# Split-operand products and a new strand order in the second mixer of a two-block transformer

## The chip, the cores and the metric

The kernel runs on one core of a Trainium2 chip. The metric is the device time of one execution in microseconds (us). Five engines work beside each other, each on its own queue: PE (TensorE, matrix products; its weight loads are counted apart as PEld), DVE (VectorE), ACT (ScalarE), POOL (GpSimd) and SP (SyncE, which issues the DMAs).

## The reference

Two blocks of two layers each run one after the other over a sequence of 512 tokens of width 1024, in float32. Each layer is a mixer and a feed-forward part; the first block has a cross-attention in between. The change touches one mixer, that of the first block's second layer. Cut to what matters:

```
proj = rms_norm(h) @ cd_w_in
lru_x, lru_g, m_x, m_o, m_if = split_cols(proj)

# y_a, gated linear recurrence, 512 channels in 4 blocks of 128
xc = causal_dwconv(lru_x, 4 taps)
r_gate, i_gate = sigmoid(xc_block @ gate_w[0 or 1] + gate_b)
log_a = -8 * r_gate * softplus(-lam)
u = sqrt(-expm1(2 * log_a)) * (i_gate * xc)
y_a = linear_recurrence(exp(log_a), u) * gelu(lru_g)

# y_b, matrix-memory head, 4 heads of 128 channels
xc = silu(causal_dwconv(m_x, 4 taps))
q, k = headwise(xc, w[0]), headwise(xc, w[1]) * 128 ** -0.5
v = headwise(m_x, w[2])
w = exp(log_d - max) * (q k^T), causal; num = w v; den = sum(w)
y_b = sigmoid(m_o) * norm(num / max(|den|, ...))

h = h + concat(y_a, y_b) @ w_mix_out
```

## The kernel before

Activations lie channel-major: a tile has 128 channels on the partitions and the 512 tokens along the free axis. A weight matrix is loaded in blocks of 128 output channels. A dense product is done as a **three-pass product** (`mm3`): each operand is split into a high part, rounded to the type `float32r`, and the remainder, and high x high, high x low and low x high are summed in PSUM. Products of smaller size are plain float32 (`mm`), which the profile shows as two records each. Splitting (`split`) is a cast on ACT and a subtraction on DVE:

```
def mm3(self, out, w, x, start, stop):
    wh, wl = w
...
    xh, xl = x
    self.mm(out, wh, xh, start, False)
    self.mm(out, wh, xl, False, False)
    self.mm(out, wl, xh, False, stop)
def split(self, src, n=T):
    hi, lo = self.big(F32R), self.big(F32R)
    self.nc.scalar.copy(out=hi[:, :n], in_=src[:, :n])
    self.tt(lo[:, :n], src[:, :n], hi[:, :n].bitcast(F32), SUB)
```

The mixer in question is `mixer_cd`. Its input projection has 17 blocks of 128 outputs: 0 the gates of the heads, 1 to 4 their input (`xm`, and after convolution and SiLU `xc`), 5 to 8 the output gate `so`, 9 to 12 the recurrence's input (after convolution `xl`), 13 to 16 its outer gate `gl`. One **dense step** is one three-pass product of 512 columns; a block has eight of them, as has each pair of blocks of a product over half the channels (`mix_out`, `kb=4`). Blocks 0, 1, 5 and 2 are the opening, under which the mean square of the input is finished.

Then `weave` takes over. It runs two **strands** at a time, each a Python generator that yields after each small piece of work: a head (`mlstm_head`: queries, keys, values, scores in four causal strips of 512, 384, 256 and 128 columns, numerator, statistics, output; 15 strand steps) or the recurrence (`rglru`: eight gate products, then exponentials, logarithms and scans; 20 strand steps). A strand starts when the other one has made 6 steps. After each strand step 1.75 dense steps of the **filler** are taken (`CD = (1.75, 6, 1)`). The filler of before is: the remaining nine blocks (`CDF[1]`, in the order 6, 3, 7, 4, 8, 9 to 12), the last part of the memory's values for the coming cross-attention (16 dense steps), blocks 13 to 16, and, once all four heads are done, the half of the output product that takes the heads' results `yb`. The strands are heads 0 to 3 and then the recurrence. What is left of the filler follows, and last comes the closing half of the output product, which takes the recurrence's result `ya`, adds the residual and prepares the next stage.

The order written in the code is a priority, not the final order of each queue: the framework's scheduler lets a later instruction go ahead of an earlier one that it expects to wait. Tiles of 128 x 512 lie in 84 shared slots (`NBIG`) that are handed on in the order in which they come free. Most instructions carry the line of a helper: L485 is every product, L475 every tensor-tensor operation, L472 every activation, L514 the cast of a loaded weight, L501 the cast of `split`, L513 a weight's DMA, L1733 the recurrence's scan.

Of the kernel before, what the change touches and what calls it, by code (L numbers as in the profile page):

```python
# [7 lines left out]
F32 = mybir.dt.float32  # L8
F32R = mybir.dt.float32r
# [8 lines left out]
T = 512  # L18
HT = T // 2
P = 128  # L20
# [327 lines left out]
class Builder:  # L348
# [1286 lines left out]
    def mlstm_head(self, h, xm, xc, rT, M, o, out):  # L1635
        nc = self.nc
        qkv = self.sm['qkv']
        hs = slice(h * P, (h + 1) * P)
        q, k, v = self.big(), self.big(), self.big()
        ps = self.ax_ps()  # L1640
        self.mm(ps, qkv[0][:, hs], xc)
        self.copy(q, ps)
        yield
        ps = self.ax_ps()
        self.mm(ps, qkv[1][:, hs], xc)
        self.act(k, ps, AF.Copy, scale=128 ** -0.5)
        yield
        ps = self.ax_ps()
        for t in range(4):
            self.mm(ps[:, t * P:(t + 1) * P], xm[:, 3 + t * P:3 + (t + 1) * P], qkv[2][:, hs])  # L1650
        self.copy(v, ps, 's')
        yield
        Mb = self.ax_ps()
        self.mm(Mb, self.c('ident')[0:4, h:h + 1].to_broadcast([4, P]), M[0:4])
        W, wsum = [], self.big()
        for sb in range(4):
            n = T - sb * P
            w = self.big()
            self.ts(w[:, :n], Mb[:, sb * P:], rT[:, 4 * sb + h:4 * sb + h + 1], SUB, 0.0, MAX)
            W.append(w)  # L1660
        yield
        for sb in range(4):
            n = T - sb * P
            w = W[sb]
            self.act(w[:, :n], w[:, :n], AF.Exp, scale=-1.0)
            self.tt(w[:, :P], w[:, :P], self.c('causal'), MULT, nc.gpsimd)
            sc = self.ax_ps()
            self.mm(sc[:, :n], k[:, sb * P:(sb + 1) * P], q[:, sb * P:])
            self.tt(w[:, :n], sc[:, :n], w[:, :n], MULT)
            if sb == 0:  # L1670
                self.copy(wsum, w, 's')
            else:
                self.tt(wsum[:, sb * P:], wsum[:, sb * P:], w[:, :n], ADD, nc.gpsimd)
            yield
        num = self.ax_ps()
        for sb in range(4):
            self.mm(num[:, sb * P:], v[:, sb * P:(sb + 1) * P], W[sb][:, :T - sb * P], sb == 0, sb == 3)
            yield
        sq, hn = self.big(), self.big()
        self.act(sq, num, AF.Square)  # L1680
        self.ts(hn, num, self.v('mng', h), MULT)
        st = self.ax_ps()
        for i, src in enumerate((wsum, sq)):
            for t in range(4):
                self.mm(st[:, 4 * i + t:4 * i + t + 1], src[:, t * P:(t + 1) * P], self.c('ones')[:, 0:1])
            yield
        d = self.small([P, 16], tag='mld')
        self.copy(d[:, 0:8], st[:, 0:8])
        self.stt(d[:, 8:12], d[:, 0:4], -1.0, d[:, 0:4], MULT, MAX)
        eT = rT[:, 16:32].rearrange("p (t h) -> p h t", h=4)[:, h]  # L1690
        self.tt(d[:, 8:12], d[:, 8:12], eT, MAX)
        self.stt(d[:, 8:12], d[:, 8:12], EPS, d[:, 8:12], MULT, MULT)
        self.stt(d[:, 8:12], d[:, 4:8], 1.0 / P, d[:, 8:12], MULT, ADD)
        self.tt(d[:, 12:16], d[:, 8:12], self.c('mhalf')[:, :4], ALU.pow, nc.gpsimd)
        yield
        self.tt(hn, hn, self.bcast(d[:, 12:16]), MULT)
        self.tt(hn, hn, o, MULT, nc.gpsimd)
        out[h] = self.split(hn)

    def rglru(self, xl, gl, lru, sp, out):  # L1700
        nc = self.nc
        rg, ig, th = [], [], []
        for n in range(4):
            cs = slice(n * P, (n + 1) * P)
            for dst, g in ((rg, 0), (ig, 1)):
                ps = self.ax_ps()
                self.mm(ps, lru[g][:, cs], xl[n])
                t = self.big()
                self.act(t, ps, AF.Sigmoid, bias=self.v(f'lgb{g}', n))
                dst.append(t)  # L1710
                yield
            t = self.big()
            self.act(t, rg[n], AF.Tanh, scale=sp[:, n:n + 1])
            self.ts(t, t, 1e-18, MAX)
            th.append(t)
            self.tt(ig[n], ig[n], xl[n], MULT, nc.gpsimd)
        for n in range(4):
            l = self.big()
            self.act(l, th[n], AF.Ln, bias=self.c('one'))
            self.act(th[n], th[n], AF.Ln, scale=2.0)  # L1720
            self.tt(th[n], th[n], l, SUB)
            yield CD[2]
        for n in range(4):
            self.act(th[n], th[n], AF.Exp, scale=0.5)
            self.act(rg[n], rg[n], AF.Exp, scale=sp[:, 4 + n:5 + n])
            self.tt(ig[n], ig[n], th[n], MULT)
            yield CD[2]
        for n in range(4):
            while n not in gl:
                yield  # L1730
            self.act(gl[n], gl[n], AF.Gelu_apprx_tanh)
            hh = self.big()
            nc.vector.tensor_tensor_scan(out=hh, data0=rg[n], data1=ig[n], initial=0.0, op0=MULT, op1=ADD)  # L1733
            self.tt(hh, hh, gl[n], MULT, nc.gpsimd)
            out[n] = self.split(hh)
            yield CD[2]

    def mixer_cd(self, filler, nxt):
        norm = self.norm_end()
        xs = self.xg  # L1740
        self.sm['qkv'] = [self.load_part('s_qkv', i) for i in range(3)]
        lru = [self.load_part('s_lru', i) for i in range(2)]
        sp = self.small([P, 16], tag='sp')
        c = self.vat['lam']
        lam = self.vec[:, c:c + 4]
        self.act(sp[:, 0:4], lam, AF.Abs)
        self.act(sp[:, 0:4], sp[:, 0:4], AF.Exp, scale=-1.0)
        self.act(sp[:, 0:4], sp[:, 0:4], AF.Ln, bias=self.c('one'))
        self.ts(sp[:, 4:8], lam, -1.0, MULT, 0.0, MAX)
        self.tt(sp[:, 0:4], sp[:, 0:4], sp[:, 4:8], ADD)  # L1750
        self.ts(sp[:, 4:8], sp[:, 0:4], -8.0, MULT)
        self.ts(sp[:, 0:4], sp[:, 0:4], 8.0, MULT)
        xm, xc, so, xl, gl, st, ya, yb = {}, {}, {}, {}, {}, {}, {}, {}

        def emit(n, ps):
            if n == 0:
                st['g'] = self.mlstm_gates(ps)
            elif n < 5:
                xm[n - 1] = self.evac_pad(ps, 3)
                xc[n - 1] = self.conv4(xm[n - 1], 'mcw', 'mcb', n - 1)  # L1760
                self.act(xc[n - 1], xc[n - 1], AF.Silu)
            elif n < 9:
                t = so[n - 5] = self.big()
                self.tt(t, ps, self.R, MULT)
                self.act(t, t, AF.Sigmoid)
            elif n < 13:
                xl[n - 9] = self.conv4(self.evac_pad(ps, 3), 'lcw', 'lcb', n - 9)
            else:
                t = gl[n - 13] = self.big()
                self.tt(t, ps, self.R, MULT)  # L1770

        def proj(blocks, groups=None):
            return self.dense_steps([self.ap['w_cd'][n] for n in blocks], xs, lambda b, ps: emit(blocks[b], ps),
                                    groups=groups)

        def mix_out(y, a, emit, groups=None, **kw):
            return self.dense_steps([self.ap['w_mo'][1][n][:, a:a + T] for n in range(8)], y, emit, groups=groups, kb=4, **kw)

        def fill():
            yield from chain(proj(CDF[1], [1] * len(CDF[1])))  # L1780
            yield from filler
            yield from chain(proj(range(13, 17), [1] * 4))
            while len(yb) < 4:
                yield
            yield from chain(mix_out([yb[h] for h in range(4)], T, self.partial))

        def head(h):
            while h not in so or h not in xc or 'g' not in st:
                next(more)
            yield from self.mlstm_head(h, xm[h], xc[h], *st['g'], so[h], yb)  # L1790

        def gated():
            while len(xl) < 4:
                next(more)
            yield from self.rglru(xl, gl, lru, sp, ya)
        more = fill()
        self.opening(proj(CDF[0], CDF[2]), norm, AT)
        self.weave([head(h) for h in range(4)] + [gated()], more, CD[0], CD[1])
        lockstep(more)
        lockstep(mix_out([ya[n] for n in range(4)], 0, self.resid(nxt), GO, closing=True))  # L1800

    def load_part(self, name, i):
        t = self.big()
# [597 lines left out]
```

## Time and profile before

| | |
|---|---|
| time, median of 3 runs | 2987.32 us (2980.75 to 2989.16) |
| the profiled execution | 2984.35 us, span 2982.2 us, mean granted clock 0.998 |
| PE busy | 2939.2 us |
| DVE busy | 2184.4 us |
| ACT busy | 1472.6 us |
| POOL busy | 240.5 us |
| HBM read | 259.53 MB, 88 GB/s over the span |

The profile is of one execution. An engine's busy time is the time covered by its instructions; a product's end is modelled, so a busy PE isn't a PE at its peak. PE's weight loads (PEld) run ahead under the products.

### The profile page before, as it was taken

The page shows a single profiled execution, that of the slowest core. Times are in us where ns is not written, and L with a number is a line of the kernel's source. Part 1 is how long each engine was busy: PE and PEld are TensorE (multiplying, and loading weights), DVE is VectorE, ACT ScalarE, POOL GpSimd, SP SyncE. Part 2 cuts the span into 40 slices and gives each one's busy share as a digit, 9 for nine tenths or more (in the row PEclk, how much of TensorE's full clock was granted, in tenths as well). Part 3 has the DMA queues.
Part 4 walks back from the last instruction along what each step waited for, and adds up shares of the span by engine and source line. Part 5 has one row for each costly group of instructions (what it writes and reads, how often), then busy time and mean ns, then how long its engine had stood idle before and what let it go on. Part 6 is the DMA issues. An engine that isn't in the chain of part 4 may idle for free.

```text
span 2982.2 us, 50430 instructions
## 1 busy us (share of the span) xinstructions
PE 2939.2 (99%) x19486; PEld 2469.8 (83%) x19486; DVE 2184.4 (73%) x3951; ACT 1472.6 (49%) x2750; POOL 240.5 (8%) x254
## 2 busy tenths in 40 slices
PE   8999999999999999999999999999999999999999
PEld 6666777889998777889998865899988888889998
DVE  6456655689887567679897656877778787788785
ACT  5344433555455566455465454454544444455452
POOL 1001100200000121100000221000001111000000
PEclk9999999999999999999999999999999999999999
DMA  4113231323324122323333112233332222323332
GB/s 138 51 47 100 65 110 54 106 67 103 103 93 127 44 89 89 97 67 105 105 95 114 57 50 89 78 96 103 98 102 68 94 77 99 114 70 111 96 98 84
DMA packets 152051, 264.91 MB, mean 89 GB/s; under 512 B 16882, under 2 KB 35970, under 8 KB 151811
## 3 DMA queue, kind: packets, MB, share of 16 engines
q1 hardware_dynamic: 151810, 261.69, 27.5%
q8 instruction: 153, 2.51, 0.3%
q14 instruction: 88, 0.71, 0.1%
HBM read 259.53 MB, written 2.10 MB: 88 GB/s over the span
## 4 chain that ended last, share of the span: by engine, by line
PE 74%; DVE 3%; issue 2%; DMA 2%; ACT 1%; POOL 1%; SPq 0%; DVEq 0%; POOLq 0%; ACTq 0%
PE pm L485 74%; DVE b L475 2%; DMA b<-in_w_up_dram 1%; POOL b L475 1%; ACT b L472 0%; ACT L472 0%; DVE b L478 0%; PE pm L1876 0%; PE pm L855 0%; DVE h L475 0%; PE pm L976 0%; DMA b<-in_w_ev_dram 0%; POOL b L482 0%; ACT b L514 0%; DMA b<-in_w_rg_dram 0%
## 5 line engine op out<-in xcount | busy, mean ns | idle before, releaser
L485 PE MATMUL pm<-b,b 128*128 128x256 f32 (+4 forms) x18412 | 2856.5, 319 | 27.5 <-DVE b L475 6.9
L485 PEld LDWEIGHTS pm<-b,b 128*128 128x128 f32 (+3 forms) x18412 | 2363.8, 176 | 444.2 <-issue 80.9
L475 DVE TENSOR_TENSOR b<-b,b 128x512 fp32r<-128x512 f32 (+3 forms) x2091 | 1323.2, 672 | 322.7 <-PE pm L485 126.0
L690 ACT CAST b<-b 128x512 fp32r<-128x512 f32 (+1 forms) x784 | 464.1, 607 | 410.9 <-PE pm L485 217.5
L514 ACT CAST b<-b 128x512 fp32r<-128x512 f32 (+2 forms) x480 | 275.1, 588 | 333.8 <-PE pm L485 46.0
L475 DVE TENSOR_TENSOR h<-pm,h 128x512 f32<-128x512 f32 x304 | 199.9, 686 | 85.2 <-PE pm L485 83.9
L475 DVE TENSOR_TENSOR b<-pm,b 128x512 f32<-128x512 f32 (+5 forms) x338 | 178.9, 540 | 98.1 <-PE pm L485 78.1
L1145 ACT COPY b<-pm 128x256 f32<-128x256 f32 (+6 forms) x391 | 145.7, 382 | 211.0 <-PE pm L485 176.6
L501 ACT CAST b<-b 128x512 fp32r<-128x512 f32 (+2 forms) x168 | 100.9, 612 | 138.5 <-DVE b L475 69.5
L472 ACT ACTIVATE b<-b 128x512 f32<-128x512 f32 (+4 forms) x215 | 124.9, 592 | 84.4 <-DVE b L475 39.0
L475 POOL TENSOR_TENSOR b<-b,b 128x512 f32<-128x512 f32 (+3 forms) x68 | 91.6, 1356 | 406.1 <-DVE b L482 138.7
L478 DVE SCALAR_TENSOR_TENSOR b<-b,vec,b 128x512 f32<-128x512 f32 (+5 forms) x149 | 107.4, 728 | 9.3 <-ACT b L472 7.6
L475 DVE TENSOR_TENSOR b<-pm,R 128x512 f32<-128x512 f32 x98 | 65.7, 686 | 42.5 <-PE pm L485 42.2
L472 ACT ACT_TABLE_LOAD x57 | 73.1, 1283 | 10.3 <-DVE mx L475 7.5
L1038 ACT CAST b<-b 128x512 fp32r<-128x512 f32 x86 | 53.2, 620 | 47.5 <-DVE b L478 43.1
L472 ACT ACTIVATE b<-h,vec 128x512 fp32r<-128x512 f32 x80 | 56.9, 715 | 38.2 <-DVE h L475 37.7
L472 ACT ACTIVATE b<-b,vec 128x512 f32<-128x512 f32 (+2 forms) x71 | 51.7, 737 | 43.4 <-DVE b L475 39.3
L485 PEld LDWEIGHTS pm<-cst,b 128*128 128x128 f32 (+3 forms) x488 | 59.4, 183 | 12.4 <-ACT b L472 3.2
L475 POOL TENSOR_TENSOR rt<-rq,cst 128x4 f32<-128x4 f32 x11 | 12.7, 1158 | 607.7 <-DVE rq L482 607.6
L478 DVE SCALAR_TENSOR_TENSOR b<-h,vec,b 128x512 fp32r<-128x512 f32 x80 | 59.4, 747 | 2.4 <-ACT b L472 1.8
L482 POOL TENSOR_SCALAR b<-b,mx 128x256 f32<-128x256 f32 (+2 forms) x48 | 45.8, 958 | 176.6 <-DVE mx L1869 58.9
L485 PE MATMUL pm<-cst,b 128*128 128x1 f32 (+4 forms) x488 | 56.7, 245 | 2.6 <-ACT b L472 1.3
(137 smaller groups left out, 838.0 us busy)
## 6 DMA issues: line engine op xcount, KB each, us to landing
b<-in_w_up_dram SPq DMA_DIRECT2D x348, 256.0 KB, 3.1
b<-in_w_dn_dram SPq DMA_DIRECT2D x96, 256.0 KB, 2.9
b<-in_w_dn_dram SPq DMA_DIRECT2D x96, 192.0 KB, 2.5
b<-in_w_cd_dram SPq DMA_DIRECT2D x34, 256.0 KB, 2.7
b<-in_w_v_dram SPq DMA_DIRECT2D x32, 256.0 KB, 2.8
b<-in_w_k_dram SPq DMA_DIRECT2D x32, 256.0 KB, 2.7
b<-in_w_q_dram SPq DMA_DIRECT2D x32, 256.0 KB, 2.8
b<-in_w_o_dram SPq DMA_DIRECT2D x32, 256.0 KB, 2.7
```

The source lines that it names most:

```text
L472: return self.nc.scalar.activation(out=out, in_=in_, func=func, bias=bias, scale=scale, **kw)
L475: return (eng or self.nc.vector).tensor_tensor(out=out, in0=a, in1=b, op=op)
L478: return self.nc.vector.scalar_tensor_tensor(out=out, in0=a, scalar=s, in1=b, op0=op0, op1=op1)
L482: return (eng or self.nc.vector).tensor_scalar(out=out, in0=a, scalar1=s1, scalar2=s2, op0=op0, **kw)
L485: return self.nc.tensor.matmul(out=out, lhsT=lhsT, rhs=rhs, start=start, stop=stop, skip_group_check=more)
L501: self.nc.scalar.copy(out=hi[:, :n], in_=src[:, :n])
L514: self.nc.scalar.copy(out=hi[:, :w], in_=raw[:, :w])
L690: self.nc.scalar.copy(out=hi[-1], in_=src)
L1038: self.nc.scalar.copy(out=hi, in_=t)
L1145: return self.nc.scalar.copy(out=out, in_=in_)
```

## The change

Queries and keys, the scores and the recurrence's gates become three-pass products. For this the weights of queries, keys and gates are split once at the start of the stage, `xc` and `xl` are split in each strand (each with a strand step of its own), and queries and keys are kept as high and low parts. The values, the numerator and the statistics stay as they are. The recurrence becomes the third strand, between heads 1 and 2. The filler takes blocks 13 to 16 before the memory's values, and the half of the output product that it takes is now that of `ya`; the closing half is that of `yb`.

```
@@ mlstm_head
-        q, k, v = self.big(), self.big(), self.big()
+        v = self.big()
+        xc = self.split(xc)
+        yield
         ps = self.ax_ps()
-        self.mm(ps, qkv[0][:, hs], xc)
-        self.copy(q, ps)
+        self.mm3(ps, self.cols(qkv[0], h * P), xc, True, True)
+        q = self.split(ps)
         yield
         ps = self.ax_ps()
-        self.mm(ps, qkv[1][:, hs], xc)
-        self.act(k, ps, AF.Copy, scale=128 ** -0.5)
+        self.mm3(ps, self.cols(qkv[1], h * P), xc, True, True)
+        k = self.big(F32R), self.big(F32R)
+        self.act(k[0], ps, AF.Copy, scale=128 ** -0.5)
+        self.stt(k[1], ps, 128 ** -0.5, k[0].bitcast(F32), MULT, SUB)
         yield
...
-            self.mm(sc[:, :n], k[:, sb * P:(sb + 1) * P], q[:, sb * P:])
+            self.mm3(sc[:, :n], self.cols(k, sb * P), self.cols(q, sb * P, n), True, True)
@@ rglru
         for n in range(4):
-            cs = slice(n * P, (n + 1) * P)
+            xn = self.split(xl[n])
+            yield
             for dst, g in ((rg, 0), (ig, 1)):
                 ps = self.ax_ps()
-                self.mm(ps, lru[g][:, cs], xl[n])
+                self.mm3(ps, self.cols(lru[g], n * P), xn, True, True)
@@ mixer_cd
-        self.sm['qkv'] = [self.load_part('s_qkv', i) for i in range(3)]
-        lru = [self.load_part('s_lru', i) for i in range(2)]
+        self.sm['qkv'] = [self.split(self.load_part('s_qkv', i)) if i < 2 else self.load_part('s_qkv', i) for i in range(3)]
+        lru = [self.split(self.load_part('s_lru', i)) for i in range(2)]
...
         def fill():
-            yield from chain(proj(CDF[1], [1] * len(CDF[1])))
+            yield from chain(proj(CDF[1], [1] * len(CDF[1])), proj(range(13, 17), [1] * 4))
             yield from filler
-            yield from chain(proj(range(13, 17), [1] * 4))
-            while len(yb) < 4:
+            while len(ya) < 4:
                 yield
-            yield from chain(mix_out([yb[h] for h in range(4)], T, self.partial))
+            yield from chain(mix_out([ya[n] for n in range(4)], 0, self.partial))
...
-        self.weave([head(h) for h in range(4)] + [gated()], more, CD[0], CD[1])
+        self.weave([head(0), head(1), gated(), head(2), head(3)], more, CD[0], CD[1])
         lockstep(more)
-        lockstep(mix_out([ya[n] for n in range(4)], 0, self.resid(nxt), GO, closing=True))
+        lockstep(mix_out([yb[h] for h in range(4)], T, self.resid(nxt), GO, closing=True))
```

## Rows read from the trace of the kernel before

**Rows 1.** The page's busy times, shares of the span and instruction counts.
```profile
PE 2939.2 (99%) x19486; PEld 2469.8 (83%) x19486; DVE 2184.4 (73%) x3951; ACT 1472.6 (49%) x2750; POOL 240.5 (8%) x254
```

**Rows 2.** Busy time by stretch: length, PE, PEld, DVE, ACT, POOL, granted clock, DMA.
```profile
960.00:984.00 24.00, 24.00 (x108) 18.87 (x107) 7.86 (x13) 7.00 (x12) 1.21 (x3) 1.00 0.25 78
...
1084.00:1101.00 17.00, 17.00 (x83) 13.44 (x82) 7.13 (x16) 5.12 (x8) 4.85 (x5) 1.00 0.28 94
1101.00:1121.00 20.00, 20.00 (x89) 14.72 (x88) 8.69 (x16) 17.40 (x21) 4.86 (x4) 1.00 0.16 53
1121.00:1141.00 20.00, 19.70 (x83) 15.34 (x83) 15.03 (x20) 18.17 (x28) 6.83 (x4) 1.00 0.32 106
1141.00:1149.00 8.00, 5.99 (x18) 3.78 (x17) 7.91 (x11) 5.49 (x11) 3.09 (x3) 0.79 0.37 118
```

**Rows 3.** The chain of waits, 1095 to 1150: start, us, what.
```profile
1137.18 3.30 DVE b L1733 x2
...
1144.62 5.46 PE pm L485 x15
```

**Rows 4.** Busy time by stretch around PE's holes and its half clock.
```profile
1141.40:1146.40 5.00, 2.98 (x9) 1.38 (x8) 5.00 (x7) 4.70 (x9) 1.41 (x2) 0.87 0.19 63
...
1072.70:1074.00 1.30, 0.58 (x3) 0.05 (x1) 0.48 (x3) 0.92 (x2) 0.71 (x1) 1.00 0.51 183
1001.60:1005.10 3.50, 3.50 (x9) 2.73 (x10) 1.28 (x4) 3.19 (x4) 0.00 (x0) 0.51 0.00 2
1145.00:1148.50 3.50, 3.50 (x9) 2.38 (x8) 3.50 (x6) 1.69 (x5) 1.28 (x1) 0.51 0.52 164
```

**Rows 5.** Busy time by stretch, each cut at starts of products.
```profile
1020.53:1023.09 2.56, 2.56 (x12) 2.07 (x11) 0.69 (x1) 2.53 (x4) 0.47 (x1) 1.00 0.00 0
1019.44:1020.53 1.09, 1.09 (x4) 0.57 (x3) 0.87 (x2) 1.07 (x2) 0.00 (x0) 1.00 0.67 214
...
1019.01:1019.44 0.43, 0.43 (x3) 0.38 (x2) 0.43 (x2) 0.42 (x2) 0.00 (x0) 1.00 0.76 248
1016.09:1016.98 0.89, 0.89 (x9) 0.89 (x8) 0.89 (x2) 0.28 (x1) 0.24 (x1) 1.00 0.00 0
2433.59:2434.29 0.70, 0.70 (x5) 0.69 (x4) 0.49 (x1) 0.00 (x0) 0.00 (x0) 1.00 0.00 0
...
1405.10:1410.06 4.96, 4.96 (x44) 4.95 (x43) 4.96 (x10) 2.54 (x6) 0.00 (x0) 1.00 0.33 116
```

**Rows 6.** Groups by line and form, 984 to 1149: busy us, mean ns, idle before.
```profile
L472 ACT ACT_TABLE_LOAD x25 | 32.1, 1283 | 0.4
L475 DVE TENSOR_TENSOR b<-b,b 128x512 fp32r<-128x512 f32 x42 | 28.8, 718 | 8.7 <-ACT b L501 6.2 <-PE pm L485 1.6 <-ACT b L514 0.9
L514 ACT CAST b<-b 128x512 fp32r<-128x512 f32 x38 | 22.4, 614 | 11.9 <-DVE b L475 4.2 <-DMA b<-in_w_cd_dram 3.0 <-DMA b<-in_w_mo_dram 1.9
...
L472 ACT ACTIVATE b<-b 128x512 f32<-128x512 f32 x28 | 17.5, 627 | 6.1 <-DVE b L482 4.4 <-DVE b L475 0.7 <-DVE b L478 0.6
...
L472 ACT ACTIVATE b<-b,sp 128x512 f32<-128x512 f32 x8 | 5.7, 713 | 0.0
L472 ACT ACTIVATE b<-pm,vec 128x512 f32<-128x512 f32 x8 | 5.4, 686 | 1.5 <-PE pm L485 1.4
L501 ACT CAST b<-b 128x512 fp32r<-128x512 f32 x8 | 5.0, 620 | 17.6 <-POOL b L475 17.5
```

**Rows 7.** Waits of the DMA queue, 905 to 1180: us in total, times, longest.
```profile
SPq L513 <- PE pm L485: 134.2, 46, 18.4
```

**Rows 8.** Groups of instructions on ACT, 1101 to 1149.
```profile
L472 ACT ACT_TABLE_LOAD x10 | 12.8, 1283 | 0.2
```

**Rows 9.** Timeline of ACT from 1101 on: start, us, instruction.
```profile
1104.44 1.15 ACT L514 CAST b<-b 128x512 fp32r<-128x512 f32 x2
1105.60 1.28 ACT L472 ACT_TABLE_LOAD   x1
1106.89 0.72 ACT L472 ACTIVATE b<-b,cst 128x512 f32<-128x512 f32 x1
```

More of the change, by code (lines that the diff above doesn't have):

```diff
@@ L1638, in mlstm_head @@
         hs = slice(h * P, (h + 1) * P)
-        q, k, v = self.big(), self.big(), self.big()
-        ps = self.ax_ps()
-        self.mm(ps, qkv[0][:, hs], xc)
-        self.copy(q, ps)
+        v = self.big()
+        xc = self.split(xc)
         yield
         ps = self.ax_ps()
-        self.mm(ps, qkv[1][:, hs], xc)
-        self.act(k, ps, AF.Copy, scale=128 ** -0.5)
+        self.mm3(ps, self.cols(qkv[0], h * P), xc, True, True)
+        q = self.split(ps)
+        yield
+        ps = self.ax_ps()
+        self.mm3(ps, self.cols(qkv[1], h * P), xc, True, True)
+        k = self.big(F32R), self.big(F32R)
+        self.act(k[0], ps, AF.Copy, scale=128 ** -0.5)
+        self.stt(k[1], ps, 128 ** -0.5, k[0].bitcast(F32), MULT, SUB)
         yield
```

## The prediction

> **What bounds the kernel now.** I read the shares of busy time first: PE 99% over the whole span [rows 1]. The change lies in one stage, the second mixer, so I cut that stage into stretches [rows 2]. PE is full in 960 to 984 and nearly so in 1084 to 1141, and loses time at the end: 5.99 of 8 us in 1141 to 1149, at a mean granted clock of 0.79. What ends last there is on the chain of waits [rows 3]: the recurrence's scans on DVE (two, 3.30 us, from 1137.18) lead to the PE run that starts at 1144.62, which is the closing product of `ya`. PE has by then used up the product of `yb`. So two things set this stage's length: the PE work itself, and, for a few us, the recurrence, which is started as fifth strand and is late. A closer cut [rows 4] prices the second: in 1141.40 to 1146.40 PE works 2.98 of 5.00 us, 2.0 idle. Behind it the granted clock stands at its half level (1.2 of 2.4 GHz): in 1145.00 to 1148.50 only 8 weight loads pass in 3.50 us, 0.44 us each, where a full-clock stretch has 11 in 2.56 us, 0.233 each [rows 5]; 8 x 0.233 = 1.9, so 1.6 us lost. End of stage: 3.6 us. An earlier hole has 0.7 us (1.30 less 0.58), and near 1002 the clock is halved once more, with 0.51 granted [rows 4].
>
> **The passes.** In [rows 5] the stretches are cut at starts of products; read the weight loads (one a record), since PE's own count adds one whose tail reaches in. One float32 product is two records. The first stretch is 11 passes of 512 columns on split operands: 0.233 us each, so a three-pass product takes 0.70. The second is one float32 product (two loads) and one such pass: 1.09 - 0.233 = 0.86. Next, 256 columns in float32: 0.43, so 384 have some 0.65. Four of 128: 0.89, so 0.22 each. A split pass has 0.70 / 4 = 0.175 at 384 columns and 4.96 / 43 = 0.115 at 256; three are 0.525 and 0.35. No split pass of 128 columns is in the trace. From 256 to 512 a pass loses 0.118, so 128 fewer columns would make it 0.06: low end 0.18 for three. High end: each pass as dear as a whole float32 product of 128, 0.66. I take 0.11 a pass, what one float32 record of that width takes with its own weight load, the nearest row: 0.33.
>
> The sum on PE: queries, keys and the eight gates are 16 products of 512, 16 x (0.86 - 0.70) = 2.6 us less. Scores per head: 0.16 + 0.125 + 0.08 less, and 0.11 more at 128 columns, 0.255 less; four heads 1.0. Together **3.6 us less** (4.2 at the low end of the 128 columns, 2.3 at the high end).
>
> The Trainium skill (FP8 and Floating Point Precision, TensorE Precision Notes) counts true FP32 as four passes. The trace agrees: 0.86 / 4 = 0.215. By that rule alone one pass of four would be saved, 3.4 us instead of 2.6 on the 16 products; the rows say a split pass is slower than a quarter of the float32 product.
>
> **The splits.** Added to ACT are casts at 0.62 us [rows 6]: 4 for weights, 4 for `xc`, 4 for `xl`, and 4 for q, whose copy used to be on DVE: 16, 9.9 us. DVE gets 4 + 4 + 4 subtractions at 0.72 [rows 6], and 4 for the keys, 11.5 us; q's subtraction replaces its copy. The weights' part (2.5 us on ACT, 2.9 on DVE) stands at the front of the stage, where ACT works 7.00 of 24 us and DVE 7.86 [rows 2], under PE's opening products: nothing. If that cover were gone it would delay the mean-square chain by up to 2.9. The other splits lie between two strands and their filler: nothing directly, but they count below. No DMA is added. Moving blocks 13 to 16 ahead of the memory values changes the order on SP's queue and not the number; SP waits 134.2 us in 46 waits for PE to free buffers [rows 7], and more live tiles (a high and a low part for weights, q, k and xc) make these longer. Which product that reaches no row says: 0 to 2 us, I take 0.
>
> **The order.** The end stall goes: `ya` is then ready a head earlier, and the closing product needs `yb` of the last head, whose tail lies under the last dense steps of `ya` and three of four k-steps of the first closing group (9 x 0.70 = 6.3 us). I take **3.6 us less**.
>
> What is late next is `ya` again, at its new place. Count dense steps (`CD[0]` = 1.75 for each strand step). Head 0 and ten steps of head 1 pull 45; then the recurrence starts, needs all four `xl`, and pulls the rest of the 72 projections at once. Until `ya` is wanted, PE then has 48 dense steps (four blocks of 8, 16 of memory values), 33.6 us; eight gates, 5.6; heads 2 and 3, each 6.4 for queries, keys, values, scores and numerator, 0.86 for a broadcast, and 20 records at 0.11 for sums and transposes, 9.5; and some 4 of head 1: **62 us**. The filler runs dry on the way: 48 / 1.75 is 27 strand steps, and up to `ya` the strands have 46 (24 of the recurrence, 6 and 16 of heads 1 and 2), so the last 19 come with no dense work that doesn't need `ya`.
>
> ACT in the same stretch [rows 6]: the recurrence's 8 sigmoids 5.4, its 8 with a decay scale 5.7, 4 more of that kind 2.9, 12 at 0.627 7.5, 8 casts 5.0: 26.5. Weight casts: 8 + 8 and 4 ahead, 20 at 0.614, 12.3. Heads 2 and 3: seven casts, copies and a square each and four exponentials, some 6 us: 12, and 1 for head 1. Table loads: 10 in the last 48 us before [rows 8], 25 in the stage [rows 6]; between 10 and 20 here (12.8 to 25.7), I take 13, as it now runs beside two heads' exponentials: 16.7. Sum **68.5 us** (64.6 to 77.5). So ACT has 6.5 us more to do than PE (2.5 to 15.5), where before, in 1084 to 1141, it had 40.7 of 57 us [rows 2]. The first two blocks of `ya`'s product take only `ya[0]` to `ya[2]` at first (6 x 0.70 = 4.2) and bridge some of it, but ACT never ran above 18.17 of 20. I take a new wait of **4.5 us** between 0 and 14 (15.5 at the top, less some bridge, with a half-clock stretch of 1.6 behind it).
>
> The Trainium skill (ScalarE: Activation LUTs, What ACT_TABLE_LOAD costs) counts a switch of tables at 1.28 us plus a drain of about 1.38. The trace shows the first without the second: a cast that ends at 1105.59, the load at 1105.60, the next activation at 1106.89 [rows 9]. By the page 13 switches would put ACT another 18 us behind; by the rows, none.
>
> **Sum:** 2984.35 (profiled execution) - 3.6 - 3.6 + 4.5 = 2981.65, 2.7 us less. The median shown is 2987.32, 3.0 above the profiled execution, so on the scale of the runs 2984.6.
>
> **Rivals.** *A, the recurrence hides wholly.* Then the new wait is 0, and the earlier hole (0.7) may close as well: 3.6 + 3.6 + 0.7 = 7.9 less, with the cheap 128 columns 8.5, and with the half-clock stretch near 1002 gone too (1.6) 10.1: 2977 to 2979. For it: by the count of steps the recurrence starts some 30 us of PE work earlier, seen from the closing product. Against: ACT's sum.
> *B, ACT becomes the bound of the stretch from the first gate to `ya`.* If it runs at its best observed share (18.17 / 20) with 20 table loads, 77.5 / 0.91 = 85 us against PE's 62: a wait of 20 after the bridge; 3.6 + 3.6 are spent, and the kernel is 13 us slower, 3000. It decides from some 7 us of wait upward (the kernel is then slower), and from 16 beyond 0.3%. For it: the filler that runs dry. Against: ACT's idle time before 1101 (5.12 of 17 busy) shows that its queue enters such a stretch with nothing behind. The Trainium skill (ScalarE: Activation LUTs, Rules for kernel authors) says to do all of one table set before switching; the new order does the opposite beside two heads, and that rule ends in B; the 25 loads of the stage [rows 6] show that the order of before doesn't follow it either.
> *C, the products get no cheaper*, if a split pass of 128 columns costs 0.66 and new weight loads stall: the order alone gives 3.6 - 4.5, +1: 2988.
>
> **How the numbers follow.** About 0.3% (9 us) is what a measurement of this kernel can tell from no change; the runs shown lie 8.4 us apart. My forecast (a wait of 2 to 10 us, so 2982 to 2990) 0.58, A 0.18, B 0.14, C 0.10. Faster by over 0.3%: most of A needs all its parts, so two thirds of it and a little of the forecast's edge, 0.15. Slower: B and little else, 0.15. Within: 0.70. The range goes from just under A's best case (2976) to the middle of B (2997).
>
> **What would show it.** Right: score and gate products of 512 columns appear as three records of 0.23; the stage's closing run starts with no idle before it; PE shows a hole before the first product of `ya`, with ACT near full. Wrong: a hole of over 10 us there or at the closing product, the latter if the last head's tail (statistics, power on POOL, broadcast, split) outlasts its cover; or 128-column passes above 0.2 us; or a second stage that changes its holes because buffers have moved.

## The result, and the profile after

The changed kernel takes 3010.24 us (median of 5 runs, 3009.57 to 3015.4), the kernel before 2985.9 beside it: 1.0082 times as long, interval 1.0069 to 1.0094. That is 24 us slower, where 2.7 us faster had been forecast, and outside the range. The profiled execution took 3009.57 us, span 3007.8, at a mean granted clock of 0.992.

The page after, the lines that answer to [rows 1] and to the table loads of [rows 6] (here of the whole program, where the kernel before has 57 loads, 73.1 us):

```profile
PE 2942.8 (98%) x19518; PEld 2478.2 (82%) x19518; DVE 2194.7 (73%) x3967; ACT 1489.6 (50%) x2773; POOL 238.4 (8%) x254
...
L472 ACT ACT_TABLE_LOAD x64 | 82.1, 1283 | 10.9 <-DVE mx L475 8.0
```

Totals hardly move: PE 3.6 us more, ACT 17. The stage shows it. Busy time by stretch, with the columns of [rows 2]:

```profile
960.00:984.00 24.00, 24.00 (x108) 18.92 (x107) 12.23 (x20) 7.11 (x13) 1.01 (x1) 1.00 0.29 88
...
1084.00:1104.00 20.00, 19.70 (x89) 15.03 (x88) 15.83 (x30) 19.12 (x35) 4.03 (x4) 1.00 0.45 140
1104.00:1124.00 20.00, 12.83 (x51) 9.37 (x49) 6.29 (x11) 19.59 (x24) 4.90 (x8) 0.74 0.26 79
1124.00:1144.00 20.00, 4.12 (x17) 3.22 (x16) 16.73 (x22) 15.00 (x24) 7.96 (x5) 0.57 0.24 79
...
1144.00:1147.20 3.20, 3.20 (x10) 2.52 (x9) 2.86 (x3) 1.13 (x3) 1.66 (x1) 0.50 0.46 162
1164.00:1184.00 20.00, 19.76 (x97) 16.02 (x96) 12.62 (x23) 7.32 (x13) 2.82 (x2) 1.00 0.29 93
```

Read PE beside ACT. From 1084 to 1124 ACT works 38.7 of 40 us, and PE loses 7.2 us in the second half of it. In the next 20 us, to 1144, PE works only 4.12 us and loses 15.9; ACT has 5 us free there and DVE works 16.73. From 1164 on PE is full again. The hole that closed the stage in [rows 4] is gone; 23 us of idle time stand ahead of 1144 in its place. PE's timeline there, with the idle time before each run and its releaser:

```profile
1099.63 11.24 PE L485 MATMUL pm<-b,b 128*128 128x512 f32 x50
1112.43 0.55 PE L485 MATMUL pm<-b,b 128*128 128x128 f32 x3 [1.57 <-DVE b L475]
1118.59 4.63 PE L485 MATMUL pm<-b,b 128*128 128x512 f32 x8 [5.61 <-DVE b L475]
1123.02 1.12 PE L485 MATMUL pm<-cst,b 128*128 128x1 f32 x8
1130.88 1.86 PE L485 MATMUL pm<-cst,b 128*128 128x1 f32 x8 [6.75 <-ACT b L472]
1139.74 1.31 PE L485 MATMUL pm<-b,b 128*128 128x512 f32 x2 [7.00 <-ACT b L501]
1143.19 1.11 PE L855 MATMUL pm<-cst,mld 128*128 128x128 f32 x4 [2.13 <-POOL mld L475]
```

Five holes, 23.1 us. The run of 8 after 5.61 us is head 2's numerator, which needs the strips of scores times exponentials, a product on DVE; the eight of one column after 6.75 us are the sums of the numerator's squares (`mlstm_head`); the first product of `ya` comes after 7.00 us, released by the split of `ya`. ACT's timeline meanwhile:

```profile
1109.43 1.28 ACT L472 ACT_TABLE_LOAD   x1
1110.73 0.52 ACT L472 ACTIVATE b<-b 128x384 f32<-128x384 f32 x1
1111.27 1.28 ACT L472 ACT_TABLE_LOAD   x1
1112.56 0.63 ACT L472 ACTIVATE b<-b 128x512 f32<-128x512 f32 x1
1113.10 0.71 ACT L472 ACTIVATE b<-b,cst 128x512 f32<-128x512 f32 x1
1113.82 1.28 ACT L472 ACT_TABLE_LOAD   x1
1115.12 0.42 ACT L472 ACTIVATE b<-b 128x256 f32<-128x256 f32 x1
1115.55 1.28 ACT L472 ACT_TABLE_LOAD   x1
...
1130.26 0.57 ACT L472 ACTIVATE b<-pm 128x512 f32<-128x512 f32 x1
```

The rows of 384 and 256 columns are head 2's exponentials, one strip each; those of 512 with `cst` are logarithms of the recurrence (`bias=self.c('one')`), those beside them the logarithms without a bias. A load stands at every change from one to the other: so the strips of 384 and 256 columns, 0.52 and 0.42 us of work, follow each other after 4.4 us. The square of the numerator, last row, runs at 1130.26, although PE has done the numerator at about 1123; it lies in ACT's queue behind the rest of the logarithms and the first exponentials of the recurrence. DVE's queue passes the delay on. The strip of 256 columns, whose exponential ends at 1115.54, is multiplied on DVE only at 1118.12, behind a subtraction of the recurrence that waits for a logarithm:

```profile
1117.51 0.69 DVE L475 TENSOR_TENSOR b<-b,b 128x512 f32<-128x512 f32 x1 [2.84 <-ACT b L472]
1118.12 0.42 DVE L475 TENSOR_TENSOR b<-pm,b 128x256 f32<-128x256 f32 x1
```

The same loads are on the chain of waits of 1080 to 1150, up to 1128.09. From there it goes over DVE and POOL, mainly the recurrence's scans (L1738), which start late because ACT was late:

```profile
1127.45 0.64 ACT b L472
...
1129.41 1.13 DVE b L1738
```

From about the first gate to about the first product of `ya`, by window and by group:

```profile
1068.00:1141.00 73.00, 51.79 (x229) 40.14 (x227) 42.77 (x73) 63.47 (x90) 19.06 (x18) 0.83 0.27 83
```
```profile
L472 ACT ACT_TABLE_LOAD x20 | 25.7, 1283 | 0.3
```

### The profile page after: what moved, and what is told of

The parts are those of the page before. It is cut to its first block, busy times and chain, and to the rows that moved or that the text cites. A ratio compares the mean times of both kernels' runs of the same rounds, so it can differ in the third digit from the quotient of the medians.

```text
span 3007.8 us, 50532 instructions
## 1 busy us (share of the span) xinstructions
PE 2942.8 (98%) x19518; PEld 2478.2 (82%) x19518; DVE 2194.7 (73%) x3967; ACT 1489.6 (50%) x2773; POOL 238.4 (8%) x254
## 4 chain that ended last, share of the span: by engine, by line
PE 73%; DVE 3%; DMA 2%; ACT 2%; issue 1%; POOL 1%; SPq 0%; DVEq 0%; ACTq 0%; POOLq 0%
PE pm L485 72%; DVE b L475 2%; DMA b<-in_w_up_dram 1%; ACT b L472 1%; ACT L472 1%; POOL b L475 1%; DVE b L478 0%; PE pm L1880 0%; DMA b<-in_w_dn_dram 0%; PE pm L855 0%; DMA b<-in_w_ro_dram 0%; PE pm L976 0%; DMA b<-in_w_ev_dram 0%; ACT b L514 0%; DVE b L1738 0%
## 5 line engine op out<-in xcount | busy, mean ns | idle before, releaser
L485 PE MATMUL pm<-b,b 128*128 128x256 f32 (+7 forms) x18444 | 2857.1, 318 | 41.3 <-DVE b L475 14.1
L485 PEld LDWEIGHTS pm<-b,b 128*128 128x128 f32 (+5 forms) x18444 | 2371.0, 176 | 452.2 <-issue 72.2
L514 ACT CAST b<-b 128x512 fp32r<-128x512 f32 (+2 forms) x480 | 275.1, 589 | 343.8 <-PE pm L485 65.6
L501 ACT CAST b<-b 128x512 fp32r<-128x512 f32 (+2 forms) x180 | 108.1, 612 | 134.3 <-DVE b L475 69.1
L472 ACT ACTIVATE b<-h,vec 128x512 fp32r<-128x512 f32 x80 | 56.9, 714 | 40.1 <-DVE h L475 39.5
```

The lines of the kernel that those rows point to most:

```text
L472: return self.nc.scalar.activation(out=out, in_=in_, func=func, bias=bias, scale=scale, **kw)
L485: return self.nc.tensor.matmul(out=out, lhsT=lhsT, rhs=rhs, start=start, stop=stop, skip_group_check=more)
L514: self.nc.scalar.copy(out=hi[:, :w], in_=raw[:, :w])
```

## The experiments

Theory T: the switches of tables beside head 2, in series with head 2's own steps, make the hole. Rival D: the filler, dry too early, makes it, with any strand. Rival F: `ya` as filler makes it, since its products now wait in the middle of the queue. The products are a question of their own: do they save the 3.6 us?

Loads are those of the whole program; PE's idle time and mean granted clock are of the window 984 to 1184 in one profiled execution (200 us less PE's busy time). Ratios are to the kernel before, run beside each; its median there lies between 2986 and 2989, so where two runs of different rows are compared below by their medians, some 3 us of the difference can be noise.

| run | median us | ratio, 95% interval | loads | PE idle | clock |
|---|---|---|---|---|---|
| before | 2985.9 | | 57 | 3.6 | 0.98 |
| after | 3010.24 | 1.0082, 1.0069 to 1.0094 | 64 | 24.9 | 0.91 |
| e1_products | 2996.56 | 1.0037, 1.0023 to 1.0052 | 60 | 11.2 | 0.93 |
| e2_order | 3005.04 | 1.0061, 1.0046 to 1.0077 | 63 | 12.4 | 0.93 |
| e3_logs | 3001.69 | 1.0049, 1.0035 to 1.0062 | 56 | 14.7 | 0.92 |
| e4_rate | 3009.83 | 1.0076, 1.0061 to 1.009 | 65 | 23.2 | 0.94 |
| e5_grouped | 2993.49 | 1.0021, 1.0009 to 1.0032 | 48 | 7.3 | 0.97 |
| e6_products_grouped | 2991.66 | 1.0012, 1.0004 to 1.0021 | 50 | 8.4 | 0.97 |
| e7_gates | 2991.27 | 1.0017, 1.0007 to 1.0027 | 58 | 6.3 | 0.98 |
| e8_heads | 2991.87 | 1.0012, 1.0001 to 1.0023 | 60 | 7.5 | 0.97 |
| e9_before_grouped | 2992.29 | 1.001, 1.0 to 1.0019 | 54 | 6.8 | 0.99 |
| e10_grouped_rate | 2994.07 | 1.0019, 1.001 to 1.0028 | 48 | 12.0 | 0.98 |
| e11_order_grouped | 2997.24 | 1.0026, 1.0013 to 1.0039 | 52 | 6.6 | 0.97 |
| e12_strand | 3019.09 | 1.0105, 1.0089 to 1.0121 | 64 | 28.7 | 0.89 |
| e13_no_tables | 2996.55 | 1.0025, 1.0016 to 1.0035 | 50 | 10.1 | 0.97 |
| e14_fourth | 2992.28 | 1.0012, 1.0002 to 1.0022 | 56 | 8.9 | 0.97 |

**Products alone, order alone.** e1_products is the kernel before with the three-pass products of the change (strands, filler and closing half as before); e2_order is the change with the products of before. Both are made of hunks of the diff shown ahead; against the kernel after, e2_order has

```
-        self.mm3(ps, self.cols(qkv[0], h * P), xc, True, True)
+        self.mm(ps, qkv[0][:, hs], xc)
...
-                self.mm3(ps, self.cols(lru[g], n * P), xn, True, True)
+                self.mm(ps, lru[g][:, cs], xl[n])
```

and so on for keys, scores and splits.

> Only the three-pass products and their splits, with the strands, the filler and the closing product in the order of before. Theory O (the new order costs the time: the recurrence beside head 2 overloads ACT while the filler is dry): faster than before by 2 to 6 us, since PE has 3.6 us less to do; score and gate passes of 512 columns at 0.23 us each. Rival P (the splits cost it: 16 more casts and as many subtractions, later buffers): slower than before by 10 us or more.

> Only the new order (recurrence as third strand, blocks 13 to 16 earlier, ya as filler, yb closing), with the plain float32 products of before. Theory O: slower than before by 20 to 30 us, with a hole on PE of some 25 us beside head 2 as in the changed kernel. Rival P: within 5 us of before.

Each part is slower by itself: 11 us for the products (0.0037 x 2986), 18 for the order. Theory O had the products faster, which is wrong, and the order slower by 20 to 30 us with a hole of some 25; PE idles 12.4 us there. With plain products the new order already has 63 loads, so the number of loads alone doesn't set the hole's length. In the new order too the products cost time: the changed kernel is 5 us behind e2_order (6 by the ratios). What they do in the old order stands mainly at the end of the stage. PE's timeline of e1_products, then a window:

```profile
1156.36 0.80 PE L485 MATMUL pm<-b,b 128*128 128x512 f32 x1 [4.25 <-ACT b L501]
1160.54 7.73 PE L485 MATMUL pm<-b,b 128*128 128x512 f32 x23 [3.38 <-DVE b L475]
```
```profile
1151.00:1165.00 14.00, 6.37 (x17) 4.32 (x16) 14.00 (x14) 8.74 (x15) 7.99 (x4) 0.64 0.42 131
```

It is the hole of [rows 3, 4], waiting for the split of `ya`: 7.6 us where it was 2.0, and behind it a longer stretch at half clock (0.64 on the mean of 14 us, DVE busy throughout). The recurrence, last strand, has become later. ACT is full ahead of it, as another window shows, where in 1121 to 1141 it had 1.8 us left [rows 2]:

```profile
1120.00:1140.00 20.00, 19.64 (x87) 15.63 (x86) 8.36 (x17) 19.78 (x25) 6.99 (x5) 1.00 0.31 93
```

More casts and three more loads are what the edit puts there. A smaller part lies earlier, where the kernel before idles 0.7 us [rows 4]; here it is 2.5 us with half clock behind it, and no run separates its cause:

```profile
1064.00:1084.00 20.00, 17.52 (x63) 11.91 (x62) 16.77 (x30) 7.50 (x14) 4.97 (x5) 0.74 0.40 118
```

**Logarithms together; a thinner filler.** In e3_logs all eight logarithms are one strand step and all eight exponentials another; empty steps behind them keep the number.

```
@@ rglru
             self.tt(th[n], th[n], l, SUB)
+        for n in range(4):
             yield CD[2]
...
             self.tt(ig[n], ig[n], th[n], MULT)
+        for n in range(4):
             yield CD[2]
```

In e4_rate a strand step takes one dense step with it in place of 1.75:

```
-CD = (1.75, 6, 1)
+CD = (1.0, 6, 1)
```

> The changed kernel, but the recurrence issues its eight logarithms in one strand step and its eight exponentials in another, with empty steps after them, so that as many dense steps are taken; the program has 56 table loads instead of 64. Theory T (the loads between the recurrence's logarithms and the heads' exponentials are what fills ACT in the hole): 8 x 1.28 = 10 us less and part of the half clock back, so 10 to 16 us faster than the changed kernel (2994 to 3000). Rival D (PE is empty because the filler has run dry, whatever ACT does): within 4 us of the changed kernel.

> The changed kernel with 1.0 instead of 1.75 dense steps for each strand step, so that the 48 dense steps that are left when the recurrence starts last for the 46 strand steps up to ya; 65 table loads. Theory D: the hole shrinks by half or more, 12 us or more faster than the changed kernel (below 2998). Theory T: ACT has the same work and loads, so the wait only moves to where the filler ends: within 6 us of the changed kernel.

e3_logs has 8 loads fewer and is 8.6 us faster than the kernel after (3001.69 against 3010.24), a little less than the 10 to 16 of theory T. e4_rate is no faster. Its windows show the hole a little earlier:

```profile
1084.00:1104.00 20.00, 16.32 (x62) 11.18 (x61) 7.27 (x13) 19.73 (x23) 4.38 (x6) 0.91 0.39 120
1104.00:1124.00 20.00, 8.04 (x23) 5.27 (x22) 14.29 (x27) 19.75 (x33) 2.00 (x3) 0.58 0.13 39
```

ACT is full in both (39.5 of 40). PE's timeline names what its longest hole waits for:

```profile
1116.26 1.22 PE L485 MATMUL pm<-b,b 128*128 128x512 f32 x2 [8.74 <-ACT b L514]
```

That is the cast of a loaded weight: dense work is left, but its weights are split on ACT too, and ACT is busy for 8.76 of the 8.80 us from 1107.50 on, first with two loads of these switches, then with activations that need none. So D falls: with filler kept back the hole moves and does not get shorter.

**The whole recurrence grouped by function.** In e5_grouped the eight gate products with their sigmoids and tanhs are one strand step too, with twelve empty ones behind. e6_products_grouped is e1_products with the same edit.

```
@@ rglru
             xn = self.split(xl[n])
-            yield
...
                 dst.append(t)
-                yield
...
             self.tt(ig[n], ig[n], xl[n], MULT, nc.gpsimd)
+        for n in range(12):
+            yield
```

(and the two hunks of e3_logs).

> The changed kernel with the recurrence's work grouped: its eight gate products with their sigmoids and hyperbolic tangents in one strand step, its eight logarithms in one, its eight exponentials in one, and empty steps behind each, so that as many dense steps are taken. The program has 48 table loads instead of 64, the same other work. Theory T (loads that alternate with the heads' exponentials fill ACT, and PE waits for it): 16 x 1.28 = 20 us of ACT less in the stretch of the hole, so the hole all but goes: 2980 to 2994. Rival D2 (the new order leaves PE without work beside head 2, however ACT is ordered): 3000 or more.

> The three-pass products alone, in the order of before, with the same grouping of the recurrence: 50 table loads instead of 60. Theory S (with the products alone, the added casts and loads on ACT make the recurrence, which ends the stage, later still): 10 x 1.28 = 13 us of ACT less, so the closing hole goes and PE's 3.6 us show: 2980 to 2988, 8 to 16 us faster than the products alone. Rival G (the split of each input in front of its gates lengthens the recurrence's own chain): within 4 us of the products alone (2996).

e5_grouped has 16 loads fewer than the changed kernel and is 16.8 us faster, as theory T had it. e6_products_grouped has 10 fewer than e1_products and is 4.9 us faster, short of the 8 to 16 of theory S: the hole at the stage's end gets shorter, but PE still idles 5.1 us in 1144 to 1164. Windows of e5_grouped:

```profile
1084.00:1104.00 20.00, 18.95 (x82) 14.73 (x81) 16.75 (x32) 19.92 (x38) 3.26 (x3) 0.91 0.30 94
1104.00:1124.00 20.00, 16.01 (x67) 11.52 (x65) 18.53 (x20) 11.79 (x21) 12.60 (x11) 0.91 0.43 127
1124.00:1144.00 20.00, 19.66 (x79) 15.39 (x80) 15.33 (x31) 10.14 (x19) 5.71 (x7) 0.83 0.26 83
```

From 1104 on ACT has 18 us free in 40, and PE loses 4.3 us in place of 23. What is busiest now is DVE, 18.53 in the second stretch.

**Which products.** e7_gates is the kernel before with three-pass gates only, e8_heads with three-pass queries, keys and scores only (the hunks of the diff for each).

> Before, with only the eight gates as three-pass products (two weights and four inputs split; 58 table loads, before 57). Theory S: six casts, 3.7 us, and one load, 1.3 us, more on ACT, 1.3 us less on PE: slower than before by 1 to 4 us. Rival G: slower by 6 to 10 us.

> Before, with only the heads' queries, keys and scores as three-pass products (two weights and four inputs split, queries and keys in two parts; 60 table loads, before 57). Theory S: ten casts, 6.2 us, and three loads, 3.8 us, more on ACT, 2.3 us less on PE: slower than before by 4 to 9 us. Rival G: within 2 us of before.

Either alone costs some 4 us (0.0017 and 0.0012 x 2987 = 5.1 and 3.6), with intervals of 2 to 8 and of 0.3 to 7, so neither run decides between the two theories. PE's timeline before the stage's end, e8_heads:

```profile
1142.81 1.26 PE L485 MATMUL pm<-b,b 128*128 128x512 f32 x4 [0.43 <-ACT b L514]
1146.54 6.93 PE L485 MATMUL pm<-b,b 128*128 128x512 f32 x22 [2.48 <-DVE b L475]
```

The closing wait is there in both (in e7_gates 1.26, 1.18 and 1.10 us follow each other): 2.9 us here and 3.5 in e7_gates, where it was 2.0 before.

**Grouping without the products, and with a thinner filler.** e9_before_grouped is the kernel before, e11_order_grouped e2_order, both with the grouped recurrence; e10_grouped_rate is e5_grouped with

```
-CD = (1.75, 6, 1)
+CD = (1.25, 6, 1)
```

> Before, with only the recurrence's work grouped as in the grouped runs (54 table loads, before 57). Theory T: 3 x 1.28 = 3.8 us of ACT less in front of the recurrence's end, which closes this stage, so part of the closing hole of 3.6 us goes: faster than before by 1 to 4 us. Rival: grouping itself (bare strand steps with dense work but no gate) costs as much: 0 to 3 us slower.

> The changed kernel with the grouped recurrence (48 table loads) and 1.25 dense steps for each strand step instead of 1.75, so that the filler lasts 38 of the 46 strand steps up to ya instead of 27. If, with ACT relieved, the dry filler is what leaves the rest of the hole (3.6 us idle at one place and 13.7 us of half clock in the grouped run): 2984 to 2990, faster than the grouped run by 3 to 8 us. If ACT's load is still the limit: within 2 us of the grouped run (2993).

> The new order with plain float32 products and the grouped recurrence (52 table loads; the order alone had 63). Theory T: 11 x 1.28 = 14 us of ACT less than the order alone, so 8 to 16 us faster than it (2989 to 2997), and within 5 us of the changed kernel with grouping: what the products save on PE (3.6 us) and what their casts cost on ACT are of one size. Rival D2: within 4 us of the order alone (3005).

The three loads saved in the kernel before bring nothing: the run is 3 us slower (1.001, interval 1.0 to 1.0019), as the rival had it. PE is not full there. At the stage's end it now idles 5.1 us in place of 2.0, as PE's timeline of e9_before_grouped shows, so the grouping has a price of its own; what makes it, no run shows:

```profile
1140.20 4.65 PE L485 MATMUL pm<-b,b 128*128 128x512 f32 x19 [0.64 <-DVE b L475]
1146.58 7.22 PE L485 MATMUL pm<-b,b 128*128 128x512 f32 x30 [1.73 <-DVE h L475]
1156.49 9.69 PE L485 MATMUL pm<-b,b 128*128 128x512 f32 x34 [2.68 <-ACT b L501]
```

In the new order 11 loads fewer bring 7.8 us (3005.04 to 2997.24; 10 by the ratios), at the lower end of the 8 to 16 of theory T. The thinner filler again does nothing (2994.07 against 2993.49).

With the grouping on both sides, the products can be judged once more. Without them it is 1.001 in the old order and 1.0026 in the new (e9_before_grouped, e11_order_grouped); with them 1.0012 and 1.0021 (e6_products_grouped, e5_grouped). The intervals overlap: the products then neither cost nor save anything that can be told, though the runs with them have 4 loads fewer.

**The strand's place alone.** e12_strand leaves the recurrence third and gives the filler and the closing product back to `yb` and `ya`:

```
-            while len(ya) < 4:
+            while len(yb) < 4:
...
-            yield from chain(mix_out([ya[n] for n in range(4)], 0, self.partial))
+            yield from chain(mix_out([yb[h] for h in range(4)], T, self.partial))
...
-        lockstep(mix_out([yb[h] for h in range(4)], T, self.resid(nxt), GO, closing=True))
+        lockstep(mix_out([ya[n] for n in range(4)], 0, self.resid(nxt), GO, closing=True))
```

> The changed kernel, but with the half of yb as filler and that of ya closing, as before: only the recurrence's place as third strand and blocks 13 to 16 ahead of the memory values remain of the order (64 table loads). Theory T (the place beside head 2 makes ACT late for head 2 and the recurrence alike): still slower than before by 15 us or more. Rival F (the deadline that ya gets as filler makes the hole): within 11 us of before, like the products alone.

It is the slowest of all, 9 us behind the kernel after (7 by the ratios) and 30 behind the kernel before, as theory T had it and not within 11 as rival F. So F falls: the hole is there without `ya` in the filler, as PE's timeline of e12_strand shows, with nearly the same three waits, and `ya` as filler is what fills PE afterwards: in 1164 to 1184, where the changed kernel works 19.76 us, e12_strand works 15.82.

```profile
1118.85 4.64 PE L485 MATMUL pm<-b,b 128*128 128x512 f32 x8 [5.61 <-DVE b L475]
...
1131.14 1.86 PE L485 MATMUL pm<-cst,b 128*128 128x1 f32 x8 [6.46 <-ACT b L472]
1140.01 0.79 PE L485 MATMUL pm<-b,b 128*128 128x512 f32 x1 [7.00 <-ACT b L501]
```
```profile
1164.00:1184.00 20.00, 15.82 (x56) 12.50 (x57) 9.41 (x15) 4.96 (x8) 2.62 (x2) 0.74 0.18 51
```

**The switches by themselves.** e13_no_tables is the changed kernel step for step, but the recurrence's sigmoids, tanhs and logarithms are replaced by the identity with the same scale and bias, so its output is not the reference's:

```
-                self.act(t, ps, AF.Sigmoid, bias=self.v(f'lgb{g}', n))
+                self.act(t, ps, AF.Identity, bias=self.v(f'lgb{g}', n))
...
-            self.act(t, rg[n], AF.Tanh, scale=sp[:, n:n + 1])
+            self.act(t, rg[n], AF.Identity, scale=sp[:, n:n + 1])
...
-            self.act(l, th[n], AF.Ln, bias=self.c('one'))
-            self.act(th[n], th[n], AF.Ln, scale=2.0)
+            self.act(l, th[n], AF.Identity, bias=self.c('one'))
+            self.act(th[n], th[n], AF.Identity, scale=2.0)
```

e14_fourth is e5_grouped with the recurrence between heads 2 and 3:

```
-        self.weave([head(0), head(1), gated(), head(2), head(3)], more, CD[0], CD[1])
+        self.weave([head(0), head(1), head(2), gated(), head(3)], more, CD[0], CD[1])
```

> The changed kernel, step for step, but the recurrence's sigmoids, hyperbolic tangents and logarithms are the identity with the same scale or bias, so that its output isn't the reference's; 50 table loads instead of 64, as many activations. If the loads fill ACT (theory T): 14 x 1.28 = 18 us of ACT less, PE's hole beside head 2 shrinks to less than 8 us and the time to 2986 to 2996. If the grouping's other order of products brought the time back: within 5 us of the changed kernel (3010).

> The changed kernel with the grouped recurrence, but as fourth strand, between heads 2 and 3 (56 table loads). If its place beside head 2, with the filler running dry, makes the grouped order's loss, then more dense steps are taken ahead of it and the time falls by 3 to 8 us against the grouped run, to 2986 to 2990. If the deadline of ya is too early there: as late as or later than the grouped run (2993 or more).

The order of the code and the number of all other instructions are those of the changed kernel; only 14 loads are missing (18.0 us of ACT), and 13.7 us of the 24 come back (17 by the ratios), at the edge of what theory T had forecast. Windows of e13_no_tables:

```profile
1084.00:1104.00 20.00, 18.39 (x76) 13.80 (x75) 14.86 (x30) 16.43 (x32) 4.77 (x4) 0.91 0.42 129
1104.00:1124.00 20.00, 15.08 (x69) 11.71 (x67) 18.56 (x25) 15.17 (x28) 12.75 (x11) 0.84 0.38 119
1124.00:1144.00 20.00, 17.98 (x77) 13.61 (x76) 17.75 (x31) 12.89 (x23) 6.94 (x9) 0.91 0.31 92
```

PE works 17.98 us in the last of these where it worked 4.12. T is shown for the larger part: PE's idle time in the stage falls from 24.9 to 10.1 us with only the loads taken away (one of the recurrence's activations with `cst` takes 0.71 us in both kernels). It is not the whole: PE still loses 8.6 us in these 60, and the time stays 0.25% above that of the kernel before. The fourth place, grouped, is 1.0012, with an interval that overlaps those of the third and of the last (e5_grouped, e6_products_grouped): once the tables are grouped, the places can't be told apart.

## Why the prediction was wrong

The step that failed is the new wait, "4.5 us between 0 and 14". It is 23 us of idle PE, and behind it a stretch at half clock. The rival that came nearest is B, held at 0.14 and priced at 3000; the run is 10 us above that. B has the direction and the 20 loads right. Its sum is not what happened: it put 77.5 us of work on ACT, where there are 63.47, and made ACT the bound up to `ya`, where from 1128 on the chain lies on DVE and POOL.

**How the wait was sized.** The table loads were taken at 13; there are 20 in 1068 to 1141, the top of the range given and what B was priced with. But the total on ACT was not under-counted: 63.47 us in those 73 against 68.5 forecast. What failed is the form of the sum. It set ACT's total against PE's total and took the difference as the wait, as if each engine could work whenever it had something to do. Even the measured totals, 63.47 less 51.79, would give 11.7 us, and PE lost 21.2. Head 2 is a chain that crosses between them: exponential (ACT), scores and numerator (PE), square (ACT), sums (PE), statistics and power (DVE, POOL). At each crossing it waited for its turn among loads and logarithms that the scheduler had put in between, and the dense work that could have stood in PE's place depends on ACT as well, for the casts of its weights (e4_rate's 8.74 us). So PE lost its 21.2 us in those 73 while ACT itself was idle for 9.5.

The holes in their order say the same. The forecast looked for a hole before the first product of `ya`, which is there (7.00 us). The 5.61 and 6.75 ahead of it are head 2's own and were in no step. e13_no_tables, e5_grouped and e3_logs say what they mainly hang on: 14, 16 and 8 loads fewer bring 13.7, 16.8 and 8.6 us (17, 18 and 10 by the ratios), about 1 us or a little more for each load of 1.28.

The Trainium skill (ScalarE: Activation LUTs, Rules for kernel authors) asks for all work of one table set before switching. The runs agree where PE waits for ACT (e5_grouped), and show no gain in the order of before (e9_before_grouped). The same section names a set that holds both exp and ln, so that the pair needs one load; the trace doesn't show that here, with a load of 1.28 us at each change between the head's exponentials and the recurrence's logarithms.

**The filler that runs dry** was given as what speaks for B. Taking it more slowly changes nothing (e4_rate, e10_grouped_rate).

**The splits, "nothing directly".** The part at the front of the stage was right: PE is full in 960 to 984 with DVE at 12.23 us in place of 7.86. The part inside the weave was wrong. e1_products has the cheaper passes and neither new strand nor new filler, and is 11 us slower: the recurrence, already what closes the stage, comes later, with more casts and three loads on ACT ahead of it, and the closing hole of 2.0 us grows to 7.6 with half clock behind. That the casts and loads make it late is read from the timeline; e6_products_grouped, with 10 loads fewer and 5.1 us idle there, supports it in part. In the new order the products add some 5 us as well (the changed kernel against e2_order).

**The passes** were right in size, as far as a row shows it. The width with no row before, 128 columns, taken at 0.11 us: two such passes cut out of the changed kernel's scores take 0.23 us, with the columns of [rows 5] (two records whose tails reach in are counted too):

```profile
1035.90:1036.13 0.23, 0.23 (x4) 0.23 (x4) 0.23 (x2) 0.05 (x1) 0.00 (x0) 1.00 0.00 0
```

PE's work did get shorter by about this much. Its busy time is 3.6 us more than before, but 28.4 us of it lie in stretches at half clock, against 13.2 before. At full clock these would have taken 14.2 and 6.6 us less, so that PE's work falls by some 4.0 us (an estimate from these two profiled executions). That the 3.6 us arrive in the time, no run shows; every run with the products is slower than the kernel before.

**The end stall** of 3.6 us went as forecast: from 1164 to 1184 PE works 19.76 us, and e12_strand, which gives that part back, is 7 to 9 us slower, so in this order the swap of the two halves is worth more than its term. **Rival A** is out; **C** is out on the passes.

**What stays open.** With the tables grouped or absent the versions with the products are still 0.1 to 0.25% slower than the kernel before (e5_grouped, e6_products_grouped, e13_no_tables, e14_fourth), where 3.6 us of PE work less should show as a gain. PE's idle time there is 4 to 7 us above that of the kernel before, and the clock 0.01 lower. The grouping without the products is as slow (e9_before_grouped, e11_order_grouped), so this can't be put down to the products alone. DVE at 18.5 of 20 us in one stretch of e5_grouped and e13_no_tables makes it a candidate, but the subtractions of the splits aren't shown to be the reason: e11_order_grouped, without them, has such a stretch too, and no run took them off DVE. And no version tried beats the kernel before.

```profile
1084.00:1104.00 20.00, 18.38 (x79) 12.79 (x78) 18.50 (x33) 17.31 (x29) 3.65 (x3) 1.00 0.57 180
```

This is e11_order_grouped.

## What to carry to other kernels

Where a strand is moved beside another, don't compare the engines' totals: write down, for the strand it now runs beside, each crossing from one engine to the other, and what may stand in the queue there. On ACT look first at which functions alternate, since each change is a load of 1.28 us in series with both strands; group them into one step before moving anything, and measure the grouping by itself: it paid where PE waited for ACT, and not in the order of before. And an operand split put on an engine that feeds the end of a stage can delay that end, even where the product itself becomes cheaper.

## What the runs showed of the hardware

In 1124 to 1144 of the changed kernel the mean granted clock is 0.57: at 0.5 for 17 of the 20 us, while PE works 4.12. It is still 0.50 in 1144.00 to 1147.20, with PE busy throughout, so the hole costs another 1.6 us there beyond its own length; the short hole of [rows 4] was followed by a loss of the same size. It also fell where PE was hardly idle: in 1004 to 1024 PE is busy for 19.74 us in the changed kernel and granted 0.83 on the mean, in e1_products the same with 19.77 us and in e2_order with all 20.00, while e5_grouped and e13_no_tables, with 19.77 each, are at 1.00:

```profile
1004.00:1024.00 20.00, 19.74 (x79) 14.01 (x78) 13.11 (x24) 12.07 (x21) 4.81 (x9) 0.83 0.13 40
```
```profile
1004.00:1024.00 20.00, 19.77 (x94) 14.55 (x95) 16.16 (x29) 15.03 (x26) 4.83 (x9) 1.00 0.14 40
```

The first is the changed kernel, the second e5_grouped. At half speed for 6.8 us that is up to 3.4 us of an execution, as much as the differences left open above, and a reason to read those from many runs and not from one profile.
